# States, down products and steps of a two-layer streaming encoder moved and merged

## The chip, the cores and the metric

The kernel runs on one core of a Trainium2 chip. The metric is the device time of one execution in microseconds, the median of several runs. TensorE (PE in the profile) multiplies matrices, VectorE (DVE) and ScalarE (ACT) work element by element, GpSimd (POOL) does small element-wise work and issues some transfers, and SyncE (SP) issues nearly all transfers between device memory and the on-chip memory. "PEld" is TensorE's loading of the stationary operand, which overlaps its products.

## The reference

Two layers of an encoder advance by one step for 512 new frames of one stream and 16 frames of each of 8 running streams: 640 rows ("tokens") of width 1024 in all. Each layer is half a feed-forward network, a mixer, and another half feed-forward network, each wrapped in a layer norm. The change touches the feed-forward network and the second mixer:

```python
def swiglu(x, w_gate, w_up, w_down):
    return (jax.nn.silu(x @ w_gate) * (x @ w_up)) @ w_down

# second mixer (mixer_ssd), after proj = x @ w_in split in z, xbc, dt_raw
conv = conv_b + sum(ext[:, w:w + length] * conv_w[w] for w in range(SSD_CONV))
xbc = jax.nn.silu(conv)

# one chunk of its recurrence (ssd_recurrence)
cs = jnp.cumsum(dt_c * a, axis=1)
seg = cs[:, :, None] - cs[:, None]
decay = jnp.exp(jnp.where(causal, seg, -jnp.inf))
cb = jnp.einsum('btgn,bsgn->btsg', c_c, b_c)
w = cb[..., None] * decay * dt_c[:, None]
y = jnp.einsum('btsgr,bsgrp->btgrp', w, x_c)
y = y + jnp.einsum('btgn,bgrpn->btgrp', c_c, h) * jnp.exp(cs)[..., None]
to_end = jnp.exp(cs[:, -1:] - cs) * dt_c
h_new = h * jnp.exp(cs[:, -1])[..., None, None] + jnp.einsum('bsgr,bsgn,bsgrp->bgrpn', to_end, b_c, x_c)

# its output
yg = y * silu(z)
yg = yg * rsqrt(mean(yg ** 2) + RMS_EPS) * norm_g
out = yg @ w_out
```

There are 32 heads in 4 groups of 8; a head's state is 64 x 128. The hidden width of the feed-forward network is 2816, which is 22 tiles of 128. The new state `h_new` of the 8 running streams is an output of its own, and nothing else uses it.

## The kernel before

The six sub-layers run one after the other as stages: ffn0, mix0, ffn1, ffn2, mix1, ffn3. Every matrix product is made in three parts: each operand is split into a high part of reduced precision and a low rest, and `mm3` (lines 129 to 135) adds high x high, low x high and high x low in one bank. `split` (93 to 96) makes the parts, a copy on ScalarE and a subtraction on VectorE. `load_w` (111 to 118) loads a weight tile on SP's queue and splits it.

**Feed-forward network** (`ffn`, from 213). The 22 hidden tiles are handled as two alone and then twenty in pairs; gate and up products of a pair are formed by a scheme of seven block products in place of eight (`matrix`, with its products at line 358). After every four hidden tiles `down` multiplies them by their rows of the down matrix. In ffn1 and ffn2, which `SEVEN` (line 31) names, four of the six down blocks run as `down7`, again seven block products in place of eight (products at line 494). It needs sums of hidden rows (`row_sums`), differences of weight rows on VectorE (468 to 471), and part of its results is added to `yacc` by accumulating transfers on GpSimd's queue (506). The fifth token tile, the first block (two hidden tiles) and the last block stay in the plain form, `tm_proj`. In ffn3 all down blocks are plain: for each of five token tiles and two halves of the width, 12 products of 512 columns.

**Second mixer** (`mixer1`, from 1473). For each of 4 groups there are six tiles of convolved projections (`xbc`) and four of gate projections (`gate_in`). They go to device memory (`bcx_d`, `z_d`) and are reread in blocks of 128 tokens. Blocks 0 to 3 of a group are the 512 new frames, in chunks; block 4 holds the 16 frames of the 8 running streams. The order of blocks in a group is 4, 0, 1, 2, 3; one block of one group is a step, and there are 20. In each step come one projection tile of the next group (`run_fill`), `core_a` for the next step's block, `core_b` (or `core_s` for block 4), another projection tile, and `gate_out` for the same block of the group before, which multiplies by the gate (`zz`, line 1767), normalizes and projects out. In the last group no projections are left to fill in. After the last step come the five `gate_out` of the last group, each with a layer norm.

`xbc` convolves by windows: the 512 frames and the 8 runs of 16 frames are separate steps on ScalarE (1554) and VectorE (1557), three taps on VectorE, then Tanh (1558) and a last step (1559). `core_a` loads `bx` and `csb`, subtracts the decay of each of 8 heads in 8 steps on VectorE (1662), takes Exp of the whole (1664), and for block 4 writes its rows of x and B, split, to `xb_d` (1691, 1692). `core_s` loads the old states of the running streams (`load_h0`) for their part of the output. `gate_out` splits its result in four steps each on ScalarE (1780) and VectorE (1781), which also scale by `norm_g`.

**New states of the running streams** (`ssd_states`, 1445 to 1471) are made beside ffn3: for each of 16 pairs of streams and groups, 12 small loads bring rows from `xb_d` to `xrow` and `brow` (1459, 1460), the old states are loaded again, one product per state tile (1467) forms the update, and VectorE multiplies the old state (1469) and adds (1470). `tick` draws a step of it at five places in ffn3's loop over pairs.

**Queues.** Every engine takes its instructions in order. `issue_after(i)` puts what is traced in its block behind `i` on the engine of `i`, without a wait of its own.

**Start.** The first product is that of ffn0, as soon as the first weight and the first columns of x are split.

Of the kernel before, what the change touches and what calls it, by code (L numbers as in the profile page):

```python
# [9 lines left out]
F32 = mybir.dt.float32  # L10
# [11 lines left out]
T = 640  # L22
# [7 lines left out]
PAIRS = 6  # L30
SEVEN = ("ffn1", "ffn2")
PHASES = ("ffn0", "mix0", "ffn1", "ffn2", "mix1", "ffn3")
# [4 lines left out]
def kernel(ctx: ExitStack, tc: tile.TileContext, I, O, phases=PHASES):  # L37
# [91 lines left out]
    def mm3(ps, lhs, rhs):  # L129
        n = 3 * len(lhs)  # L130
        k = 0
        for (wh, wl), (xh, xl) in zip(lhs, rhs):
            for a, b in ((wh, xh), (wl, xh), (wh, xl)):
                state["pe"] = nc.tensor.matmul(ps, a, b, start=(k == 0), stop=(k == n - 1)).ins  # L134
                k += 1


# [75 lines left out]
    def ffn(i, ph, last, side=None):  # L213
# [4 lines left out]
        with ExitStack() as st:  # L218
# [1216 lines left out]

    ssd = {}

    def load_h0(wk, g, j):
# [3 lines left out]

    def ssd_states(wk):

        el8 = wk.tile([128, 4, 8, 8], F32, name="el8")
        nc.sync.dma_start(el8.rearrange("p g b h -> p g (b h)"), ssd["el"])


        xrow = wk.tile([128, 512], F32R, name="xrow", bufs=1)
        brow = wk.tile([128, 2, 128], F32R, name="brow", bufs=1)  # L1450
        nc.vector.memset(xrow.bitcast(F32), 0.0)
        nc.vector.memset(brow.bitcast(F32), 0.0)
        for g, b2, q in ((g, b2, q) for g in range(4) for b2 in range(2) for q in range(2)):
            for h in range(2):
                for r, (sx, sb) in enumerate(((0, 0), (0, 1), (1, 0))):
                    rows = slice(64 * h + 16 * r, 64 * h + 16 * r + 16)
                    t0 = 64 * h + 32 * b2 + 16 * q
                    src = lambda s, a, b: ssd["xb"][g][s, t0:t0 + 16, a:b]
                    nc.sync.dma_start(xrow[rows].bitcast(F32), src(sx, 0, 512))
                    nc.sync.dma_start(brow[rows, h].bitcast(F32), src(sb, 512, 640))  # L1460
            for h in range(2):
                n = 4 * h + 2 * b2 + q
                h0 = wk.tile([128, 512], F32, name="h0", bufs=2)
                nc.sync.dma_start(h0, I["ssd_h0"][g, n])
                yield
                pst = bank_b()
                nc.tensor.matmul(pst, brow[:, h], xrow, start=True, stop=True)  # L1467
                h4 = h0.rearrange("p (h d) -> p h d", d=64)
                nc.vector.tensor_tensor(h4, h4, el8[:, g, n, :, None].to_broadcast([128, 8, 64]), op=ALU.mult)
                nc.vector.tensor_tensor(h0, h0, pst, op=ALU.add)  # L1470
                nc.sync.dma_start(O["ssd_s"][g, n], h0)

    def mixer1(ph, last):
        V, G = nc.vector, nc.gpsimd
        cs_d = dram.tile([32, T], F32, name="cs_d")
        bcx_d = [dram.tile([128, NT, 6, 128], F32, name=f"bcx_d{g}") for g in range(4)]
        el_d = ssd["el"] = dram.tile([128, 4, 64], F32, name="el_d")
        xb_d = ssd["xb"] = [dram.tile([2, 128, 640], F32, name=f"xb_d{g}") for g in range(4)]
        z_d = [dram.tile([128, NT, 4, 128], F32, name=f"z_d{g}") for g in range(4)]
        with ExitStack() as st:  # L1480
# [58 lines left out]
            def xbc(g, u):  # L1539
                for h in range(0 if (g, u) not in xin else 1, 2):  # L1540
                    xbc_half(g, u, h)
                _, ext, m = xin[g, u]
                es_ = ext[:, 515:667].rearrange("p (b i) -> p b i", i=19)
                if u == 0:
                    cvo[g] = wk.tile([128, 6, 27], F32, name="cvo", bufs=1)
                G.tensor_copy(cvo[g][:, u, 0:3], ext[:, 512:515])
                G.tensor_copy(cvo[g][:, u, 3:27].rearrange("p (b i) -> p b i", i=3), es_[:, :, 16:19])
                if u == 5:
                    nc.sync.dma_start(O["conv"][:, 6 * g:6 * g + 6], cvo[g])
                acc = row_tile("acc")[:, :T]  # L1550
                win = lambda w: ((ext[:, w:w + 512], acc[:, 0:512]),
                                 (es_[:, :, w:w + 16], acc[:, 512:640].rearrange("p (b i) -> p b i", i=16)))
                for i_, o_ in win(0):
                    nc.scalar.activation(o_, i_, AF.Identity, scale=cw[:, m, 0:1], bias=cw[:, m, 4:5])
                for w in range(1, 4):
                    for i_, o_ in win(w):
                        V.scalar_tensor_tensor(o_, i_, cw[:, m, w:w + 1], o_, op0=ALU.mult, op1=ALU.add)
                nc.scalar.activation(ext[:, :T], acc, AF.Tanh)
                V.scalar_tensor_tensor(acc, ext[:, :T], 1.0, acc, op0=ALU.add, op1=ALU.mult)
                nc.sync.dma_start(bcx_d[g][:, :, u, :], acc.rearrange("p (c t) -> p c t", t=128))  # L1560

# [67 lines left out]

            bl = {}  # L1630

            def core_a(g, c):
                bx = wk.tile([128, 6, 128], F32, name="bx", bufs=2)
                nc.sync.dma_start(bx, bcx_d[g][:, c])
                bt, ct, xs = bx[:, 0], bx[:, 1], bx[:, 2:6]
# [9 lines left out]
                else:  # L1645
                    e8 = wk.tile([128, 8, 8], F32, name="e8")
                    nc.scalar.activation(e8.rearrange("p b h -> p h b"),
                                         csb.rearrange("p h (b i) -> p h b i", i=16)[:, :, :, 15], AF.Exp)
                    nc.sync.dma_start(el_d[:, g], e8.rearrange("p b h -> p (b h)"))
                ecs = None  # L1650
# [7 lines left out]
                elif c == 4:  # L1658
                    ecs = wk.tile([128, 8], F32, name="ecs8")
                    nc.scalar.activation(ecs, tok[:, c, 0, hs], AF.Exp)  # L1660
                for h in range(8):
                    V.tensor_scalar(csb[:, h, :], csb[:, h, :], tok[:, c, 0, 8 * g + h:8 * g + h + 1], 0.0,
                                    op0=ALU.subtract, op1=ALU.min)
                nc.scalar.activation(csb, csb, AF.Exp)
                pcb = bank_b()
# [64 lines left out]
            def core_s(g, c):  # L1730
# [9 lines left out]
                for j in range(4):  # L1740
                    h0 = load_h0(wk, g, j)
# [17 lines left out]
            def gate_out(g, c):  # L1759
                if g not in wo:  # L1760
                    wo[g] = [load_w(I["m1_out"][4 * g + k]) for k in range(4)]
                y = ys.pop((g, c))
# [14 lines left out]
                og = wk.tile([128, 4, 2, 128], F32R, name="csb" if g == 3 and c % 2 else "og", bufs=2 if g == 3 and c % 2 else 1)  # L1777
                for q in range(4):
                    ng = chp[:, 1, 4 * g + q:4 * g + q + 1]
                    nc.scalar.mul(og[:, q, 0], y[:, q], ng)  # L1780
                    V.scalar_tensor_tensor(og[:, q, 1], y[:, q], ng, og[:, q, 0].bitcast(F32),  # L1781
                                           op0=ALU.mult, op1=ALU.subtract)
                for j in range(2):
# [68 lines left out]

    open_banks()
    if "mix0" in phases and "ffn0" not in phases:
        with ExitStack() as st:
# [3 lines left out]
    if "mix0" in phases and "ffn0" in phases:  # L1859
        sides["ffn0"] = s5_tables  # L1860
    if "mix1" in phases and "ffn3" in phases:
        sides["ffn3"] = ssd_states
    for ph in phases:
# [5 lines left out]
        else:  # L1869
            mixer1(ph, last)  # L1870
            if "ffn3" not in phases:
                with ExitStack() as st:
                    for _ in ssd_states(pool("ssd", 1, st, reuse_waits="tile")):
                        pass
    banks[-1].close()
# [111 lines left out]
```

## Time and profile before

| | us |
|---|---|
| median of 3 runs | 2548.34 (2546.8 to 2552.1) |
| profiled execution, its time | 2548.97 |
| profiled execution, its span | 2547.3 |
| ffn0, from the span's start to its layer norm | 0 to 432 |
| second mixer with its layer norm | about 1597 to 2113 |
| ffn3 from there to its last down block | 2113 to 2511 |
| last down block and layer norm | 2511 to 2547 |

The page has engine totals, the chain of work that ended last, and groups of equal instructions with their mean duration and the idle time before them. The windows give each engine's busy time in a stretch. A matmul's duration contains its way through the array; what it costs in a dense stream is the distance from one start to the next, which is shorter. In the chain and the timeline the first number is the start in us from the span's start and the second is the length in us.

### The profile page before, as it was taken

To read this page: it belongs to the slowest core of one execution; us is meant where nothing else is said; L and a number is where in the kernel's file an instruction comes from. 1 tells how busy PE (TensorE), PEld (TensorE's weight loads), DVE (VectorE), ACT (ScalarE), POOL (GpSimd) and SP (SyncE) were. 2 spreads that over 40 slices of the span, in tenths; PEclk is the share of its full clock that TensorE was granted. 3 is DMA by queue.
4 is the path that set the end of the run, shared out by engine and by line. 5 is a ranking of instruction groups with operands and counts; after the bars stand their busy time and mean duration, and the time that the engine had idled before them with its cause. 6 is when DMAs were issued, how large, how long until landed. Compare 5 with 4: busy or idle time off the path is not lost. (4 is left out here: it accounts for less than half of the span.)

```text
span 2547.3 us, 40681 instructions
## 1 busy us (share of the span) xinstructions
PE 2501.8 (98%) x15577; PEld 2289.1 (90%) x15577; DVE 2017.0 (79%) x3685; ACT 1218.0 (48%) x2309; POOL 298.3 (12%) x432
## 2 busy tenths in 40 slices
PE   9999999999999999999999999999999999999998
PEld 8998999878789999999999999888989879999997
DVE  7787777676778888878888887777686799876768
ACT  4443344336744555553455554566565443443332
POOL 0000001210130000013000002311111150000001
PEclk9999999999999999999999999999999999999999
DMA  5322334443221433452144434366564722543442
GB/s 185 108 92 86 114 117 154 143 150 114 87 76 58 125 103 91 117 156 72 53 114 123 112 103 127 117 189 196 155 204 142 240 74 85 168 147 107 145 140 96
DMA packets 174835, 317.44 MB, mean 125 GB/s; under 512 B 20480, under 2 KB 91776, under 8 KB 174128
## 3 DMA queue, kind: packets, MB, share of 16 engines
q1 hardware_dynamic: 164816, 293.83, 36.2%
q0 software_dynamic: 9824, 21.01, 4.0%
q8 instruction: 122, 2.00, 0.3%
q14 instruction: 73, 0.60, 0.1%
HBM read 259.56 MB, written 40.54 MB: 118 GB/s over the span
## 5 line engine op out<-in xcount | busy, mean ns | idle before, releaser
L96 DVE TENSOR_TENSOR w<-raw,w 128x512 fp32r<-128x512 f32 (+1 forms) x601 | 524.1, 897 | 74.6 <-ACT w L95 73.3
L95 ACT CAST w<-raw 128x512 fp32r<-128x512 f32 (+1 forms) x601 | 441.7, 776 | 286.5 <-PE bank L134 102.7
L358 PE MATMUL bank<-xhi,w 128*128 128x320 f32 x2432 | 540.0, 309 | 1.5 <-ACT mx L369 1.1
L134 PE MATMUL bank<-xhi,w 128*128 128x256 f32 (+2 forms) x2272 | 497.3, 311 | 8.2 <-ACT w L95 6.2
L134 PE MATMUL bank<-w,h 128*128 128x512 f32 x1872 | 436.8, 392 | 0.0
L358 PE MATMUL bank<-T,w 128*128 128x320 f32 x2736 | 426.3, 309 | 1.1 <-DVE s L395 0.7
L134 PEld LDWEIGHTS bank<-w,h 128*128 128x128 f32 x1872 | 350.3, 188 | 73.2 <-DVE h L96 1.0
L358 PEld LDWEIGHTS bank<-xhi,w 128*128 128x128 f32 x2432 | 407.4, 188 | 5.4 <-ACT mx L369 2.3
L358 PEld LDWEIGHTS bank<-T,w 128*128 128x128 f32 x2736 | 406.4, 188 | 3.0 <-DVE s L395 1.3
L134 PEld LDWEIGHTS bank<-xhi,w 128*128 128x128 f32 x2272 | 377.6, 188 | 19.5 <-ACT w L95 6.2
L358 PE MATMUL bank<-xlo,w 128*128 128x320 f32 x1216 | 375.1, 308 | 0.0
L134 PE MATMUL bank<-xlo,w 128*128 128x256 f32 (+2 forms) x1136 | 350.6, 309 | 3.0 <-DVE xlo L198 2.9
L358 PEld LDWEIGHTS bank<-xlo,w 128*128 128x128 f32 x1216 | 228.0, 188 | 0.3
L134 PEld LDWEIGHTS bank<-xlo,w 128*128 128x128 f32 x1136 | 213.8, 188 | 4.4 <-DVE xlo L198 3.6
L210 DVE SCALAR_TENSOR_TENSOR yacc<-bank,yacc 128x512 f32<-128x512 f32 x160 | 109.3, 687 | 76.7 <-PE bank L134 76.2
L369 ACT COPY mx<-bank 128x320 f32<-128x320 f32 x228 | 96.5, 424 | 140.5 <-PE bank L358 140.1
L96 DVE TENSOR_TENSOR w<-sw,w 128x1024 fp32r<-128x1024 f32 x76 | 93.0, 1224 | 53.4 <-ACT w L95 53.0
L95 ACT CAST w<-sw 128x1024 fp32r<-128x1024 f32 x76 | 79.9, 1051 | 98.1 <-DVE sw L337 96.9
L506 POOL DMA_DIRECT2D yacc<-ev x56 | 48.7, 903 | 644.6 <-ACT ev L505 587.8
L134 PE MATMUL bank<-w,og 128*128 128x512 f32 x432 | 104.8, 396 | 2.8 <-DVE og L1781 2.8
L134 PEld LDWEIGHTS bank<-w,og 128*128 128x128 f32 x432 | 79.5, 188 | 20.7 <-DVE og L1781 4.7
L397 ACT ACTIVATE s<-s 128x320 f32<-128x320 f32 x108 | 50.9, 471 | 83.6 <-DVE s L395 83.4
(428 smaller groups left out, 3468.0 us busy)
## 6 DMA issues: line engine op xcount, KB each, us to landing
raw<-in_w_gate_dram SPq DMA_DIRECT2D x88, 512.0 KB, 3.9
raw<-in_w_up_dram SPq DMA_DIRECT2D x88, 512.0 KB, 4.0
raw<-in_w_down_dram SPq DMA_DIRECT2D x88, 512.0 KB, 3.6
raw<-in_m_in_dram SPq DMA_DIRECT2D x52, 512.0 KB, 4.5
yacc<-ev POOLq DMA_DIRECT2D x56, 256.0 KB, 4.3
raw<-in_m_out_dram SPq DMA_DIRECT2D x24, 512.0 KB, 4.1
csb<-cs_d SPq DMA_DIRECT2D x20, 512.0 KB, 5.0
h<-in_ssd_h_dram SPq DMA_DIRECT2D x16, 512.0 KB, 6.2
```

The lines of the kernel that those rows point to most:

```text
L95: nc.scalar.copy(hi, src)
L96: return nc.vector.tensor_tensor(lo, src, hi.bitcast(F32), op=ALU.subtract)
L134: state["pe"] = nc.tensor.matmul(ps, a, b, start=(k == 0), stop=(k == n - 1)).ins
L210: state["acc"] = nc.vector.scalar_tensor_tensor(ya, pb, scale, ya, op0=ALU.mult, op1=ALU.add).ins
L358: nc.tensor.matmul(ps, A[p][:, a, k * 128:k * 128 + 128], B[p][b][:, k, :], start=(first and n == 0), stop=(n == 11), skip_group_check=True)
L369: nc.scalar.copy(e[n], ps)
L397: state["silu"] = nc.scalar.activation(t, ps, AF.Silu).ins
L506: nc.gpsimd.dma_start(yacc[:, t, 512 * j:512 * j + 512], e, accum_op=ALU.add)
```

## The change

- ffn3 joins the stages with seven-product down blocks; the steps beside it go.
- The new states are made in the mixer: `states_in` loads rows, in the step of block 4 for four streams and in the step of block 1 for the other four, into two pairs of `xrow` and `brow`; `states_new` makes four states in the steps of block 0 and of block 2, from the old states that `core_s` loaded; `states_out` stores them a step later. Loads and stores stand behind the load of a block (`state["bx"]`) on SP's queue. The decay factors stay on the chip.
- The convolution runs over all 664 positions at once; positions between runs hold values that nothing reads. The result of the running streams goes to a tile of its own, and there are two stores.
- The eight decay subtractions become one, and the minimum with 0 becomes Relu on ScalarE.
- `norm_g` moves into the output weights (`load_w` with `rows`); the split of the gate's result is one step on each engine.
- Eleven products of the identity with itself stand ahead of the first product.

```diff
-SEVEN = ("ffn1", "ffn2")
+SEVEN = ("ffn1", "ffn2", "ffn3")
...
-    def load_w(src):
+    def load_w(src, rows=None):
...
-            split(w[:, j, 0], w[:, j, 1], r[:, 512 * j:512 * j + 512])
+            half = r[:, 512 * j:512 * j + 512]
+            if rows is None:
+                split(w[:, j, 0], w[:, j, 1], half)
+            else:
+                nc.scalar.mul(w[:, j, 0], half, rows)
+                nc.vector.scalar_tensor_tensor(w[:, j, 1], half, rows, w[:, j, 0].bitcast(F32),
+                                               op0=ALU.mult, op1=ALU.subtract)
...
-                state["pe"] = nc.tensor.matmul(ps, a, b, start=(k == 0), stop=(k == n - 1)).ins
+                with tc.issue_after(state["first"]) if "first" in state else ExitStack():
+                    state["pe"] = nc.tensor.matmul(ps, a, b, start=(k == 0), stop=(k == n - 1)).ins
...
-                elif ph == "ffn3" and where in ("gate", "up", 0, 2, 4):
-                    with tc.issue_after(state["silu"]):
-                        next(steps, None)
...
-                acc = row_tile("acc")[:, :T]
-                win = lambda w: ((ext[:, w:w + 512], acc[:, 0:512]),
-                                 (es_[:, :, w:w + 16], acc[:, 512:640].rearrange("p (b i) -> p b i", i=16)))
-                for i_, o_ in win(0):
-                    nc.scalar.activation(o_, i_, AF.Identity, scale=cw[:, m, 0:1], bias=cw[:, m, 4:5])
+                acc = row_tile("acc")
+                n = 664
+                nc.scalar.activation(acc[:, :n], ext[:, :n], AF.Identity, scale=cw[:, m, 0:1], bias=cw[:, m, 4:5])
                 for w in range(1, 4):
-                    for i_, o_ in win(w):
-                        V.scalar_tensor_tensor(o_, i_, cw[:, m, w:w + 1], o_, op0=ALU.mult, op1=ALU.add)
-                nc.scalar.activation(ext[:, :T], acc, AF.Tanh)
-                V.scalar_tensor_tensor(acc, ext[:, :T], 1.0, acc, op0=ALU.add, op1=ALU.mult)
-                nc.sync.dma_start(bcx_d[g][:, :, u, :], acc.rearrange("p (c t) -> p c t", t=128))
+                    V.scalar_tensor_tensor(acc[:, :n], ext[:, w:w + n], cw[:, m, w:w + 1], acc[:, :n],
+                                           op0=ALU.mult, op1=ALU.add)
+                nc.scalar.activation(ext[:, :n], acc[:, :n], AF.Tanh)
+                runs = lambda t: t[:, 515:667].rearrange("p (b i) -> p b i", i=19)[:, :, :16]
+                last_ = wk.tile([128, 128], F32, name="cvs", bufs=2)
+                V.scalar_tensor_tensor(last_.rearrange("p (b i) -> p b i", i=16), runs(ext), 1.0, runs(acc),
+                                       op0=ALU.add, op1=ALU.mult)
+                V.scalar_tensor_tensor(acc[:, :512], ext[:, :512], 1.0, acc[:, :512], op0=ALU.add, op1=ALU.mult)
...
+            def states_in(g, j):
+                x, b = xrow[j % 2], brow[j % 2]
+                for h in range(2):
+                    for r, (sx, sb) in enumerate(((0, 0), (0, 1), (1, 0))):
+                        rows = slice(64 * h + 16 * r, 64 * h + 16 * r + 16)
+                        t0 = 16 * (2 * j + h)
+                        with tc.issue_after(state["bx"]):
+                            nc.sync.dma_start(x[rows].bitcast(F32), xb_d[g][sx, t0:t0 + 16, 0:512])
+                            nc.sync.dma_start(b[rows, h].bitcast(F32), xb_d[g][sb, t0:t0 + 16, 512:640])
...
+            def states_new(g, j):
+                h0 = h0s.pop((g, j))
+                for h in range(2):
+                    n = 2 * j + h
+                    pst = bank_b()
+                    nc.tensor.matmul(pst, brow[j % 2][:, h], xrow[j % 2], start=True, stop=True)
+                    V.tensor_tensor(by_head(h0[:, h]), by_head(h0[:, h]), decay[g][:, n, :, None].to_broadcast(hb3),
+                                    op=ALU.mult)
+                    V.tensor_tensor(h0[:, h], h0[:, h], pst, op=ALU.add)
+                made.append((g, j, h0))
...
-                for h in range(8):
-                    V.tensor_scalar(csb[:, h, :], csb[:, h, :], tok[:, c, 0, 8 * g + h:8 * g + h + 1], 0.0,
-                                    op0=ALU.subtract, op1=ALU.min)
-                nc.scalar.activation(csb, csb, AF.Exp)
+                V.tensor_tensor(csb, csb, tok[:, c, 0, hs, None].to_broadcast([128, 8, 128]), op=ALU.subtract)
+                nc.scalar.activation(csb, csb, AF.Relu, scale=-1.0)
+                nc.scalar.activation(csb, csb, AF.Exp, scale=-1.0)
...
-                for q in range(4):
-                    ng = chp[:, 1, 4 * g + q:4 * g + q + 1]
-                    nc.scalar.mul(og[:, q, 0], y[:, q], ng)
-                    V.scalar_tensor_tensor(og[:, q, 1], y[:, q], ng, og[:, q, 0].bitcast(F32),
-                                           op0=ALU.mult, op1=ALU.subtract)
+                split(og[:, :, 0], og[:, :, 1], y)
...
+                states_out()
                 (core_b if c < 4 else core_s)(g, c)
+                if c == 1:
+                    states_in(g, 2)
+                    states_in(g, 3)
                 run_fill(0 if i in (8, 14) else 1)
+                if c == 4:
+                    states_in(g, 0)
+                    states_in(g, 1)
+                elif c in (0, 2):
+                    states_new(g, c)
+                    states_new(g, c + 1)
...
+    pw = bank_b()
+    for _ in range(11):
+        state["first"] = nc.tensor.matmul(pw[:, 0:128], ident, ident, start=True, stop=True).ins
```

More of the change, by code (lines that the diff above doesn't have):

```diff
@@ L133, in mm3 @@
             for a, b in ((wh, xh), (wl, xh), (wh, xl)):
-                state["pe"] = nc.tensor.matmul(ps, a, b, start=(k == 0), stop=(k == n - 1)).ins
+                with tc.issue_after(state["first"]) if "first" in state else ExitStack():
+                    state["pe"] = nc.tensor.matmul(ps, a, b, start=(k == 0), stop=(k == n - 1)).ins
                 k += 1
+        state.pop("first", None)
     xt = {n: act.tile([128, KT, T], F32R, name="x" + n) for n in ("hi", "lo")}
@@ L1441, in load_h0 @@
         return h0
[L1443 to L1471, printed above, removed]
     def mixer1(ph, last):
@@ L1476, in mixer1 @@
         bcx_d = [dram.tile([128, NT, 6, 128], F32, name=f"bcx_d{g}") for g in range(4)]
-        el_d = ssd["el"] = dram.tile([128, 4, 64], F32, name="el_d")
-        xb_d = ssd["xb"] = [dram.tile([2, 128, 640], F32, name=f"xb_d{g}") for g in range(4)]
+        xb_d = [dram.tile([2, 128, 640], F32, name=f"xb_d{g}") for g in range(4)]
         z_d = [dram.tile([128, NT, 4, 128], F32, name=f"z_d{g}") for g in range(4)]
@@ L1648, in core_a @@
                                          csb.rearrange("p h (b i) -> p h b i", i=16)[:, :, :, 15], AF.Exp)
[L1649 removed]
+                    decay[g] = e8
                 ecs = None
@@ L1760, in gate_out @@
                 if g not in wo:
-                    wo[g] = [load_w(I["m1_out"][4 * g + k]) for k in range(4)]
+                    wo[g] = [load_w(I["m1_out"][4 * g + k], chp[:, 1, 4 * g + k:4 * g + k + 1]) for k in range(4)]
                 y = ys.pop((g, c))
@@ L1870 @@
             mixer1(ph, last)
[L1871 to L1874, printed above, removed]
     banks[-1].close()
```

23 lines of the change are left out of this document (17 added, 6 removed).

## Prediction

> **What bounds the kernel now.** First the page: engine totals and the chain that ended last.
>
> ```profile
> span 2547.3 us, 40681 instructions
> PE 2501.8 (98%) x15577; PEld 2289.1 (90%) x15577; DVE 2017.0 (79%) x3685; ACT 1218.0 (48%) x2309; POOL 298.3 (12%) x432
> PE 15%; DVE 2%; DMA 0%; issue 0%; ACT 0%; POOLq 0%; DVEq 0%; ACTq 0%
> ```
>
> TensorE is busy for 98% of the span, and the chain of waits, as far as it reaches back, is mostly TensorE. So a removed product is worth its place in the stream, and a removed VectorE step is worth something only where TensorE stands idle. Next the windows, by stage: the second mixer and its end, then ffn2 and ffn3 between the same two marks (from the transposes of the last token tile of the norm before, to the first product of the last down block).
>
> ```profile
> 1610.00:2060.00 450.00, 444.58 (x2953) 400.53 (x2952) 336.59 (x763) 256.75 (x726) 73.09 (x162) 1.00 0.57 179
> 2060.00:2113.33 53.33, 50.15 (x284) 42.59 (x284) 48.80 (x95) 23.73 (x46) 29.82 (x29) 1.00 0.18 56
> 1187.83:1566.97 379.14, 378.76 (x2290) 357.67 (x2289) 321.96 (x497) 196.14 (x311) 25.41 (x30) 1.00 0.39 106
> 2113.33:2511.34 398.01, 396.49 (x2370) 372.98 (x2369) 309.02 (x488) 155.16 (x265) 1.15 (x2) 1.00 0.42 134
> ```
>
> The columns are length, then busy time of PE, PEld, DVE, ACT, POOL. ffn2 does with VectorE busy for 85% (321.96 of 379.14) and leaves TensorE 0.4 us idle. The second mixer leaves 5.4 us idle in 450 and 3.2 in its end. These idle times are all that VectorE's relief can win there.
>
> **ffn3 by seven products.** ffn2 is the price list: same sizes, already in the new form. TensorE's rows of the same two windows, by line: the plain product helper in ffn2 and ffn3, the seven-product line in ffn2, the state products in ffn3.
>
> ```profile
> 1187.83:1566.97 379.14, 67.44 (x350) 59.90 (x349) 1.00 0.39 106
> 2113.33:2511.34 398.01, 156.47 (x734) 132.15 (x733) 1.00 0.42 134
> 1187.83:1566.97 379.14, 77.95 (x336) 62.76 (x336) 1.00 0.39 106
> 2113.33:2511.34 398.01, 12.54 (x32) 6.00 (x32) 1.00 0.42 134
> ```
>
> ffn3 runs 734 plain products; ffn2 runs 350 and 336 in the new form, 686. That is 48 fewer: four down blocks, each 84+24 in place of 120. ffn3 also loses the 32 state products. What one costs in the stream is read from the chain, in order of time:
>
> ```profile
> 2385.12 10.88 PE bank L134 x48
> 2396.00 0.23 PE bank L1467
> ```
>
> 10.88/48 = 0.227 us for a product of 512 columns, 0.23 for a state product. So 48 x 0.227 = 10.9 and 32 x 0.23 = 7.4, together 18.3 us. The windows say the same: 398.01 - 379.14 = 18.9; the remaining 0.6 is idle time (1.5 us of TensorE in ffn3's window, 0.4 in ffn2's). I take **-18.9**. Its bounds are -18.3 (the idle time stays) and -18.9. What ffn3 gains in VectorE work (sums, differences, splits) and in accumulating transfers on POOL is what ffn2 carries already with 0.4 us of idle TensorE; if that cover were gone it would show there. The state steps' VectorE work leaves ffn3.
>
> **States in the second mixer.** The 32 products come back there, into a stage with TensorE 98.8% busy: 32 x 0.23 = **+7.4**. Around them:
>
> ```profile
> L1469 DVE TENSOR_TENSOR h<-h,el 128x512 f32<-128x512 f32 x32 | 21.9, 685 | 1.6 <-DMA h<-in_ssd_h_dram 0.9 <-DVE h L1470 0.7
> L1470 DVE TENSOR_TENSOR h<-h,bank 128x512 f32<-128x512 f32 x32 | 21.8, 680 | 8.7 <-PE bank L1467 8.7
> L1662 DVE TENSOR_SCALAR csb<-csb,tok 128x128 f32<-128x128 f32 x160 | 34.3, 282 | 16.7 <-ACT e L1647 9.6 <-ACT el L1644 6.9
> L1670 DVE TENSOR_TENSOR csb<-csb,cbm 128x1024 f32<-128x1024 f32 x20 | 24.7, 1235 | 0.3
> L1781 DVE SCALAR_TENSOR_TENSOR og<-yb,chp,og 128x128 fp32r<-128x128 f32 x72 | 27.3, 426 | 5.0 <-ACT og L1780 5.0
> L1557 DVE SCALAR_TENSOR_TENSOR acc<-ext,cw,acc 128x512 f32<-128x512 f32 (+1 forms) x144 | 69.2, 548 | 17.7 <-POOL cvo L1547 8.6 <-ACT acc L1554 8.0 <-DMA raw<-in_m_in_dram 1.1
> L1559 DVE SCALAR_TENSOR_TENSOR acc<-ext,acc 128x640 f32<-128x640 f32 x24 | 19.7, 819 | 2.1 <-ACT ext L1558 2.0
> L1664 ACT ACTIVATE csb<-csb 128x1024 f32<-128x1024 f32 x20 | 21.2, 1058 | 23.9 <-DVE csb L1662 16.7 <-DVE rms L1775 7.1
> ```
>
> VectorE, as recorded. States: +(21.9+21.8) = +43.7. Decay differences: eight of 282 ns become one of 1235, 20 x (2.26-1.24) = -20.4. Output split: four of 426 become one of about 685 (a 512-wide step, first row), 20 x (1.70-0.69) = -20.2. Convolution: a tap's two steps (512 and 128 wide, 2 x 548 ns) become one step of 664 columns, by the 640-wide row about 0.84, and the last step's 819 becomes two, 2 x 548: 24 x (3 x 0.26 - 0.28) = -12.0. Sum -8.9. Records of short steps overlap; were half of the 52.6 saved such overlap, the sum would be +17. So -9 to +17, on 336.6 of 450: 73 to 79%, below ffn2's 85%. ScalarE gains the Relu, 20 x 1.06 = 21 us, on 57%. Both are covered by TensorE's stream in groups 0 to 2; in the last group, without projections left to fill in, they lie bare. TensorE's longest wait in this stage, the total with its count and the longest piece:
>
> ```profile
> PE bank L134 <- DVE og L1781: 2.8, 3, 2.1
> ```
>
> The 2.8 falls in the last gate steps, where VectorE is nearly full and the merged split is shorter: between -2.8 (all goes) and +5.5, if the four state renewals of the last group's third block (4 x 1.37 on VectorE) all land ahead of a gate step. The row nearest is the merged split's own saving of 1.0 per block against one such wait of 2.1; I take **-0.7**. The norm scale moved into the weights puts the same number of steps of the same width on the same engines: nothing.
>
> **The transfers.** The 32 loads of old states beside ffn3 go, the mixer's own load is used again. The 192 small row loads move into the mixer, on SP's queue, 24 at a time, in the first and third steps of each group, behind the load of a block.
>
> ```profile
> L1459 SPq DMA_DIRECT2D xrow<-xb_d x96: 302/418/982, 2113.7 to 2470.2; - x96
> ...
> 1836.79 0.32 SPq L1767 DMA_DIRECT2D zz<-z_d  x1
> ...
> 1852.87 0.38 PE L1773 MATMUL bank<-ones,zz 128*128 128x2 f32 x2
> ...
> 2028.74 0.60 SPq L1767 DMA_DIRECT2D zz<-z_d  x1
> ...
> 2034.86 0.68 DVE L1768 TENSOR_TENSOR yb<-yb,zz 128x512 f32<-128x512 f32 x1
> ...
> 2039.33 0.38 PE L1773 MATMUL bank<-ones,zz 128*128 128x2 f32 x2
> ```
>
> 24 x 0.418 = 10.0 us of SP. Behind them can stand the gate's load (zz), weight loads, and stores. From zz's issue to the use on TensorE it is 16.1 us in a step of an earlier group and 10.6 in the last group; there the first use on VectorE comes 6.1 after the issue. Weight loads have four buffers ahead and the SP queue mostly waits for VectorE to free them. The row loads themselves wait for products a whole step back; their own products come about a step later, so TensorE should find the rows there. Bounds: 0 (hidden) to +23.6 (below); near is the first, since most gate loads have more than 10 us. I take **+1.0**.
>
> **Identity products.** The start, TensorE unless marked:
>
> ```profile
> 1.26 0.28 POOL masks.py:199 TENSOR_SCALAR_AFFINE_SELECT ident<-ident 128x128 f32<-128x128 f32 x1
> ...
> 11.31 0.63 PE L134 MATMUL bank<-xhi,w 128*128 128x256 f32 x2
> 11.74 0.41 PE L134 MATMUL bank<-xlo,w 128*128 128x256 f32 x1
> 11.95 0.58 PE L134 MATMUL bank<-xhi,w 128*128 128x256 f32 x2
> ...
> 12.49 0.39 PE L134 MATMUL bank<-xhi,w 128*128 128x256 f32 x2
> 12.72 0.28 PE L134 MATMUL bank<-xlo,w 128*128 128x256 f32 x1
> 12.83 0.39 PE L134 MATMUL bank<-xhi,w 128*128 128x256 f32 x2
> ...
> 9.32 2.42 ACT L95 CAST w<-raw 128x512 fp32r<-128x512 f32 x4 [0.65 <-DMA raw<-in_w_up_dram]
> 9.97 2.58 DVE L96 TENSOR_TENSOR w<-raw,w 128x512 fp32r<-128x512 f32 x4 [0.57 <-ACT w L95]
> ```
>
> Three products take 0.64 us up to 11.95 and 0.34 after it: half rate from the first product (6.15 us) for 5.8 us. The page's clock row says full speed there and doesn't show it. With the identity ready at 1.54, products can run before 6.15. But the second weight's first low half is ready only at 9.97 + 0.64 = 10.6, so its 24 products (8 x 0.34 = 2.7) end at 13.3 in place of 11.95 + 2.7 = 14.7: **-1.35**, held later, as the next weights have us of slack. Bounds: 0 (the identity, mostly zeros, doesn't raise the clock) and -2.9 (all of the cold half).
> [...]
>
> **Sum.** -18.9 + 7.4 - 0.7 + 1.0 - 1.35 = -12.55. The profiled execution took 2548.97 (span 2547.3, 1.7 around it): 2536.4. The median of the runs is 2548.34, 0.6 lower, and the runs spread over 5.3; I forecast **2536.0**.
>
> **Rivals.**
> 1. *Waits of a few us in the mixer's last group* (for: VectorE is nearly full there, 48.8 of 53.3; against: only two blocks take new states there). The 4 x 1.37 = 5.5 us bare in place of -0.7: 2542. Chance 0.20.
> 2. *SP's queue becomes the bound; slower than before.* The 24 transfers go ahead of the gate's load each time. In groups 1 and 2, of the 16.1 us from issue to use, the landing and the gate's own steps take about 8 (an estimate: the last group's 10.6, of which 6.1 are spent up to the first use, taken as 2 more than the landing needs), so a 10.0 us delay costs about 1.9, four times; in the last group 8, twice: 7.6 + 16 = 23.6 in place of 1.0, giving 2558.6. It decides from 13.6 us of stalls, 2.3 us in each of the six steps. For it: the queue takes its transfers in one order. Against: in the rows above the gate's load is issued ahead of the next block's load at times, so the order follows readiness. Chance 0.07.
> 3. *More than forecast:* VectorE's relief removes the waits for og and most of the 5.4 us idle: 3.5 to 5 us better, 2531.5. Against: part of that idle is the norm at the mixer's start. Chance 0.14.
> 4. *Relu doesn't share ScalarE's table with Exp and Tanh.* A load is 1.28 us:
>
> ```profile
> 11.76 1.28 ACT L273 ACT_TABLE_LOAD   x1
> ```
>
> Two per block put 2.6 us on each block's decay chain; bare in four blocks of the last group and in four latency-bound others, 20 us: 2556. Against: Copy, Identity and Square run today between Tanh and Exp, without loads in the groups. Chance 0.02.
> [...]
>
> **Chances and range.** Forecast 0.57, rivals 0.20, 0.07, 0.14, 0.02. About 0.2%, 5 us, is what can be told from no change: faster means below 2543.2. Forecast, rival 3 and about three quarters of rival 1 lie there: 0.86; same 0.06 (the rest of rival 1, milder stalls); slower 0.08. The range, 2529.5 to 2544.0, takes in rivals 1 and 3 with the spread of the runs, and leaves out 2 and 4 and their milder forms.
>
> **What would show it.** Right: ffn3 between its marks at about 379 us, with 336 products on the seven-product line and 350 plain ones; mixer from its first product to the same mark 7 to 8 us longer; full rate of TensorE from its first projections. Wrong: TensorE waiting in the mixer for state rows, for zz or for decay tiles; table loads in the blocks; ffn3 longer than ffn2. If the mixer grows by over 20 us, SP's queue took the gain.

## The result, and the profile after

The changed kernel takes 2612.94 us (median of 4 runs, 2611.73 to 2613.75), the kernel before 2548.2 in runs beside it: a ratio of 1.0253, 95% interval 1.0241 to 1.0266. It is slower by 65 us; 12 us faster was forecast.

From the page of the changed kernel, engine totals, the row of the granted clock in 40 slices, and the chain:

```profile
span 2610.0 us, 40449 instructions
PE 2508.9 (96%) x15551; PEld 2291.2 (88%) x15551; DVE 2045.2 (78%) x3511; ACT 1261.6 (48%) x2289; POOL 337.2 (13%) x464
PEclk9999999999999999999999999998989889999999
PE 29%; DVE 4%; DMA 2%; ACT 2%; POOL 1%; SPq 1%; issue 1%; POOLq 0%; DVEq 0%; ACTq 0%
```

TensorE is busy 7 us longer in all, though it has fewer products, and its share fell from 98 to 96%. The dips of the clock row (slices 28 to 33) all lie in the second mixer. The windows show where the time went: from ffn2's last down block to the transposes of the mixer's last token tile, and from there to ffn3's last down block. Columns: start and end, length, busy time of PE, PEld, DVE, ACT and POOL, granted clock, DMA share, GB/s. First before, then after:

```profile
1566.97:2113.33 546.36, 534.53 (x3461) 477.32 (x3460) 419.42 (x920) 298.27 (x798) 128.57 (x217) 1.00 0.51 158
2113.33:2511.34 398.01, 396.49 (x2370) 372.98 (x2369) 309.02 (x488) 155.16 (x265) 1.15 (x2) 1.00 0.42 134
```

```profile
1559.97:2195.03 635.06, 560.00 (x3493) 494.41 (x3492) 434.86 (x738) 304.48 (x736) 143.41 (x221) 0.94 0.50 156
2195.03:2574.27 379.24, 378.90 (x2291) 357.72 (x2290) 321.08 (x496) 193.67 (x307) 25.28 (x30) 1.00 0.38 104
```

ffn3 gave what was forecast: 379.24 - 398.01 = -18.8. Up to the mixer 7.0 us are won (1559.97 against 1566.97); the experiments below whose start is the same reach that mark at 1560.9 to 1564.8, so part of the 7.0 is spread between executions. The mixer grew by 88.7, and ate both: -7.0 + 88.7 - 18.8 - 0.2 (the end) = +62.7, the difference of the spans. In the mixer TensorE stands idle for 75.1 us (635.06 - 560.00) where it stood 11.8. The waits of TensorE, total, times and longest, name most of it:

```profile
PE bank L1785 <- POOL zz L1784: 54.3, 5, 17.6
PE bank L141 <- ACT w L121: 11.1, 1, 11.1
```

Five waits for the gate's squares (zz) and one for an output weight. The longest, in the timeline of all engines (start, length; in brackets the idle time before, and who ended it). Line numbers are those of the changed kernel: 1623 and 1624 are the row loads, 1779 the load of zz, 1647 that of bx, 1780 the product with the gate, 1781 and 1784 the squares and their sum, 1785 the product that adds them up.

```profile
2102.06 1.09 PE L1731 MATMUL bank<-csb,xd 128*64 128x128 f32 x16
2103.32 0.60 SPq L1623 DMA_DIRECT2D xrow<-xb_d  x1
2103.96 0.42 SPq L1624 DMA_DIRECT2D brow<-xb_d  x1
...
2113.83 0.42 SPq L1623 DMA_DIRECT2D xrow<-xb_d  x1
2114.30 0.42 SPq L1624 DMA_DIRECT2D brow<-xb_d  x1
2114.81 0.37 SPq L1779 DMA_DIRECT2D zz<-z_d  x1
2115.29 0.36 SPq L1647 DMA_DIRECT2D bx<-bcx_d  x1
...
2117.61 0.69 DVE L1780 TENSOR_TENSOR yb<-yb,zz 128x512 f32<-128x512 f32 x1 [10.21 <-DMA zz<-z_d]
2118.39 0.63 ACT L1781 ACTIVATE zz<-yb 128x512 f32<-128x512 f32 x1 [8.68 <-DVE yb L1780]
...
2120.74 0.59 PE L1785 MATMUL bank<-ones,zz 128*128 128x2 f32 x2 [17.59 <-POOL zz L1784]
```

From 2103.32 to 2114.72 SP issues nothing but row loads. Only then come the gate's load and the next block's, and behind zz's landing stand VectorE, ScalarE, GpSimd and at last TensorE. The wait's row names GpSimd, but the first in the line is the load.
These are 20 of the burst's 24 loads; its first was issued at 2096.5. From the first row load to the last, the six bursts that stand ahead of a gate's load take 18 to 23 us, not the 10.0 of 24 issues, because other transfers stand between the row loads, and some of them wait. In the burst from 2041.25 to 2064.38 the largest such wait of SP is for VectorE, ahead of two stores of gate projections (line 1555; the 8.2 is the total of the two):

```profile
SPq L1555 <- DVE acc L1548: 8.2, 2, 5.0
```

### The profile page after: what moved, and what is told of

Read it like the earlier page. It is cut to its first block, busy times and chain, and to the rows that moved or that the text cites. A ratio compares the mean times of both kernels' runs of the same rounds, so it can differ in the third digit from the quotient of the medians.

```text
span 2610.0 us, 40449 instructions
## 1 busy us (share of the span) xinstructions
PE 2508.9 (96%) x15551; PEld 2291.2 (88%) x15551; DVE 2045.2 (78%) x3511; ACT 1261.6 (48%) x2289; POOL 337.2 (13%) x464
## 5 line engine op out<-in xcount | busy, mean ns | idle before, releaser
L96 DVE TENSOR_TENSOR w<-raw,w 128x512 fp32r<-128x512 f32 (+2 forms) x569 | 520.3, 937 | 73.7 <-ACT w L95 72.7
L141 PE MATMUL bank<-w,h 128*128 128x512 f32 x1488 | 346.3, 391 | 0.0
L141 PEld LDWEIGHTS bank<-w,h 128*128 128x128 f32 x1488 | 276.9, 188 | 57.1 <-DVE h L96 1.0
L511 POOL DMA_DIRECT2D yacc<-ev x84 | 72.8, 892 | 965.9 <-ACT ev L510 884.4
L499 PE MATMUL bank<-w,hs 128*128 128x512 f32 x576 | 132.5, 389 | 0.0
L141 PE MATMUL bank<-w,og 128*128 128x512 f32 x432 | 118.9, 431 | 12.3 <-ACT w L121 11.1
L499 PEld LDWEIGHTS bank<-w,hs 128*128 128x128 f32 x576 | 108.1, 188 | 22.5
L141 PEld LDWEIGHTS bank<-w,og 128*128 128x128 f32 x432 | 89.1, 211 | 32.6 <-ACT w L121 11.8
```

Of the source, the lines that this page charges most:

```text
L96: return nc.vector.tensor_tensor(lo, src, hi.bitcast(F32), op=ALU.subtract)
L499: nc.tensor.matmul(ps, a[:, u], b[:, v], start=(first and n == 0), stop=(n == 5), skip_group_check=True)
L511: nc.gpsimd.dma_start(yacc[:, t, 512 * j:512 * j + 512], e, accum_op=ALU.add)
```

## The experiments

The kernel before, run beside each group of these, took 2546.7 to 2547.3 us. "The stretch" below is the mixer's window between the same two marks as above (546.4 before, 635.1 after).

### The row loads left out

```diff
-                for h in range(2):
+                for h in range(0):
                     for r, (sx, sb) in enumerate(((0, 0), (0, 1), (1, 0))):
```

> The changed kernel with the 192 row loads left out (the new states are then made of cleared rows; their values are not the reference's); products, VectorE steps, loads of old states and stores stay. Theory A (the row loads fill SP's queue, and the gate's load, the output weights and the block loads stand behind them): the stretch from ffn2's last down block to ffn3's last transposes falls from 635 to 550-556 us, the time to 2526-2534, waits of TensorE for zz near 0. Rival B (VectorE's 64 renewal steps and the longer decay chain with Relu make TensorE wait): the stretch stays above 610, the time above 2590.

One run: 2541.07 us. And the states left out altogether (`states_in`, `states_new`, `states_out` not called):

> The changed kernel with the new states of the running streams left out altogether (no row loads, products, VectorE steps or stores). A: 32 products of 0.23 us less than the run without row loads, so 2519-2527. B: near 2520 too, but then far below the run without row loads. Rival C (the merged steps themselves, the decay chain with Relu above all, slow the mixer): above 2560.

2526.62 us, ratio 0.9922 (0.9905 to 0.9938), so the rest of the change is worth 20 us. The stretch, with the row loads left out and with the states left out:

```profile
1564.21:2124.44 560.23, 545.03 (x3494) 485.13 (x3493) 432.33 (x738) 301.83 (x736) 160.90 (x221) 1.00 0.54 170
```

```profile
1560.88:2108.34 547.46, 534.71 (x3462) 478.32 (x3461) 395.11 (x674) 302.07 (x736) 144.89 (x221) 1.00 0.51 159
```

This splits the 88.7: +1.1 without states (547.46 against 546.36), +12.8 for the 32 products with their VectorE steps and stores (560.23), and **+74.8 for the 192 row loads** (635.06). Of the last, 59.9 is idle time of TensorE (75.1 against 15.2) and 15.0 is busy time for the same number of products, at a clock of 0.94 in place of 1.00. Leaving the loads out came 7 us above what was expected of it, since the 12.8 were taken for less.

### The same loads elsewhere in order, or on another queue

Queued behind the gate's load of their block:

```diff
-                        with tc.issue_after(state["bx"]):
+                        with tc.issue_after(state["zz"] if g else state["bx"]):
...
-                nc.sync.dma_start(zz, z_d[g][:, c])
+                state["zz"] = nc.sync.dma_start(zz, z_d[g][:, c]).ins
```

(`states_in` is called after `gate_out` for it.)

> The changed kernel with the same 192 row loads, traced after the gate's load of their step and put behind it on SP's queue. A, as an order of single loads: TensorE's waits for zz fall from 54 to under 15 us, the time to 2530-2560. Rival D (the small transfers load the DMA engines and so slow every other transfer, wherever they stand): the waits stay, above 2590.

2582.4 us, ratio 1.0137 (1.0122 to 1.0152): 30 us better than the change, but short of what was expected. TensorE's waits:

```profile
PE bank L141 <- ACT w L95: 10.0, 3, 4.6
PE bank L1785 <- POOL zz L1784: 8.2, 3, 4.0
PE bank L1678 <- DMA bx<-bcx_d: 4.4, 4, 1.7
```

zz fell from 54.3 to 8.2, and weights and bx are late in its place, as they would be if whatever stands behind the burst pays. The three rows are 22.6 of the 40.2 us for which TensorE stands idle in this run's stretch (602.19 - 561.97); 15.2 of idle time are there without row loads too.

Issued by ScalarE in place of SP:

```diff
-                            nc.sync.dma_start(x[rows].bitcast(F32), xb_d[g][sx, t0:t0 + 16, 0:512])
-                            nc.sync.dma_start(b[rows, h].bitcast(F32), xb_d[g][sb, t0:t0 + 16, 512:640])
+                        nc.scalar.dma_start(x[rows].bitcast(F32), xb_d[g][sx, t0:t0 + 16, 0:512])
+                        nc.scalar.dma_start(b[rows, h].bitcast(F32), xb_d[g][sb, t0:t0 + 16, 512:640])
```

> The changed kernel with the same row loads issued by ScalarE in place of SP. A: SP's queue is free and the gate's load in time; 192 issues of about 0.4 us take 80 us of ScalarE (58% busy in the mixer, then about 73%): 2530-2560. D: the transfers are the same, so above 2590.

2608.09 us, ratio 1.0237 (1.0222 to 1.0252). By its number this spoke against the queue as the cause. Its waits and its timeline say why it doesn't (line 1779 is here the product with the gate, on VectorE, and 1780 the squares, on ScalarE):

```profile
PE bank L1784 <- POOL zz L1783: 43.3, 4, 14.6
```

```profile
2098.22 0.69 DVE L1779 TENSOR_TENSOR yb<-yb,zz 128x512 f32<-128x512 f32 x1 [0.64 <-DMA zz<-z_d]
...
2106.47 0.63 ACT L1669 ACTIVATE ecs<-ecs 128x512 f32<-128x512 f32 x1 [5.76 <-DMA ecs<-cs_d]
2106.49 0.31 ACTq L1623 DMA_DIRECT2D brow<-xb_d  x1
...
2111.76 0.43 ACTq L1622 DMA_DIRECT2D xrow<-xb_d  x1
2112.23 0.43 ACTq L1623 DMA_DIRECT2D brow<-xb_d  x1
2112.70 0.63 ACT L1780 ACTIVATE zz<-yb 128x512 f32<-128x512 f32 x1 [5.60 <-DMA brow<-xb_d]
```

The gate's load is in time now, and the squares' input is ready at 2098.91, but the squares start only at 2112.70: in ScalarE's own order they stand behind the issues of the burst, and behind a load of ecs for which ScalarE waited 5.76. The block moved from the load of zz to its use. The theory had been told too narrowly: not SP's queue alone, but ScalarE's stream as well, when it carries the burst ahead of something that TensorE waits for (54.3 us of waits for zz with the burst on SP, 43.3 on ScalarE).
Issue time is what matters in this case: a row load takes 0.42 us to issue (median of 96, on SP) and 1.9 to land, and 24 of them stand in a line.

### Number of transfers against bytes

One load of 320 KB a pair (the expectation's 328, in the unit of its 240): the rows are stored already in the order of the product's partitions, with 8 stores a group in place of 2. A stream's product then runs over 64 partitions in place of 128 half cleared, and 16 that were cleared hold low x low.

```diff
+                    for k in range(4):
+                        nc.sync.dma_start(xb_d[g][:, k, :, 0:512], xs_[:, k // 2].bitcast(F32))
+                        nc.sync.dma_start(xb_d[g][:, k, :, 512:640], bs_[:, k % 2].bitcast(F32))
...
+                with tc.issue_after(state["bx"]):
+                    nc.sync.dma_start(xrow[j % 2].bitcast(F32),
+                                      xb_d[g][2 * j:2 * j + 2].rearrange("n k i c -> (n k i) c"))
```

> The split rows are stored in the order in which a step needs them (8 stores of a row group in place of 2), so that one load of 328 KB brings a pair's rows in place of 12 loads of 240 KB together: 16 row loads in all instead of 192, for more bytes. Theory Q (what costs is the number of transfers issued in order on a queue on which the gate's loads, the weights and the next block's loads also stand, 0.4 us each): 2536 to 2548 us, near the 2541 of the kernel without row loads, and no wait for zz over 3 us. Theory T (what costs is the traffic, that is bytes, engines or device memory): as slow as the change or slower, 2595 to 2625.

And the same layout and bytes, with that load cut into 12 (six ranges of rows, two of columns):

> As the run before, same layout and the same bytes, but the one load of a pair is cut into 12 by rows and columns, so 192 row loads stand on SP's queue again. Theory Q: the time returns to that of the change, 2595 to 2620 us, with waits of TensorE for zz of 10 us and over. Theory T (bytes), or that the scattered rows of the first layout were slow: within 8 us of the run before.

One load: 2578.48 us, ratio 1.0121 (1.0104 to 1.0139). Cut in 12: 2645.12 us, 1.0387 (1.0371 to 1.0402). TensorE's wait for zz, first of one load, then of 12:

```profile
PE bank L1777 <- POOL zz L1776: 15.9, 3, 8.6
```

```profile
PE bank L1779 <- POOL zz L1778: 58.3, 5, 16.7
```

At equal bytes, 176 more transfers cost 66.6 us, 0.38 each, close to the 0.42 of an issue: the number decides that much. But neither time was as expected: one load stays 37 us above the 2541 without row loads, and cut in 12 it is 32 us above the change. So this form costs some 30 us by itself, with few loads and with many. It stores twice the bytes with four times the stores (32 in all, which take SP 0.83 and 0.61 us each to issue, medians of 16) and loads a third more; which of these costs it was not tried.

### Fewer loads, smaller bursts

Four loads a pair from the change's own layout (partitions ordered by part, then stream; GpSimd masks the two streams apart), all else as in the change:

```diff
+                    nc.sync.dma_start(x[0:64].bitcast(F32), rows(0, 0, 512, [[0, 2]]))
+                    nc.sync.dma_start(x[64:96].bitcast(F32), rows(1, 0, 512, []))
+                    nc.sync.dma_start(b[0:64, 0].bitcast(F32), rows(0, 512, 128, [[128 * 640, 2]]))
+                    nc.sync.dma_start(b[64:96, 0].bitcast(F32), rows(0, 512, 128, []))
+                for h in (1, 0):
+                    G.tensor_scalar_mul(b[:, h], b[:, 0].bitcast(F32), half[:, h:h + 1])
```

> The change's layout in device memory and its 240 KB a pair kept, at the same places, but brought by 4 loads a pair in place of 12 (the partitions in another order, so that a load covers 32 or 64 of them; GpSimd then masks the two streams of a pair apart). 64 row loads in place of 192, bursts of 8 in place of 24. Theory Q (what stands in the way is the count of transfers issued in order): between the 2541 without row loads and the 2613 with 192 by their number, about 2565, 2555 to 2575. Theory T (bytes and device memory): 2600 and over.

2570.56 us, ratio 1.009 (1.0074 to 1.0105), as expected of the number. Then both with the four loads and with the change's twelve, one pair's rows a block and two products in the next:

```diff
-                if c == 4:
-                    states_in(g, 0)
-                    states_in(g, 1)
-                elif c in (0, 2):
-                    states_new(g, c)
-                    states_new(g, c + 1)
+                if c < 4:
+                    states_new(g, c)
+                if c != 3:
+                    states_in(g, (c + 1) % 5)
```

> As the run before, and one pair's rows a block (a burst of 4 loads, 1.7 us) with that pair's two products in the block after, in place of two pairs at once. Theory Q with slack (a burst costs only what exceeds the time by which zz is early): 2543 to 2556, at best 3 us faster than the kernel before. If the loss goes by the number of loads alone, it stays where the run before is, within 5 us.

> The change with its 12 loads a pair kept, but one pair's rows a block (bursts of 12, 5 us) and two products a block, as in the run before; 192 loads and the same bytes. Theory Q with slack: less is lost than in the change, 2565 to 2595, since a burst holds the gate's load back for half as long. If the number alone decides: 2605 to 2620.

Both leave out the store of the last pair of states of the last group (512 KB). Four loads spread: 2555.1 us, 1.0032 (1.0021 to 1.0043). Twelve loads spread: 2584.72 us, 1.0146 (1.0129 to 1.0163). Twelve loads at once and twelve spread are the same 192 transfers with the same bytes, in bursts of 24 and of 12; the second costs 28 us less. So the number of loads alone does not tell the loss; that a burst costs only what exceeds the time that its followers have to spare fits these times, but the spare time itself was not measured. Rival D, as it was put (above 2590 wherever the transfers stand), is out: the two kernels in which SP issues the 192 loads in another place or in smaller bursts took 2582.4 and 2584.72. A smaller cost of the transfers themselves is not excluded. TensorE's waits for zz follow the loss: four loads at once, twelve spread and four spread are 29, 44 and 14 us above the 2541 without row loads, the change 72 with 54.3 of waits.

```profile
PE bank L1793 <- POOL zz L1792: 26.7, 3, 15.1
PE bank L1785 <- POOL zz L1784: 38.5, 6, 11.9
PE bank L1793 <- POOL zz L1792: 6.7, 2, 4.7
```

Last, the four loads spread, with that store added, and beside it the same with the row loads queued behind the gate's load:

> Four loads a pair, one pair a block, as in the run of that order, with the one store added that was left out there (the states of the last pair of the last row group, 512 KB): 2553 to 2559 us, so 0.2 to 0.5% slower than the kernel before. It makes the best form of the change so far whole.

> As the run beside it, and the row loads are queued behind the gate's load of the same block. Theory Q: the 6.7 us of waits for zz go and up to 7 us are gained, 2546 to 2555, at best level with the kernel before. Rival (what is put behind the gate's load now holds back the next block's loads, as in the earlier run of that order): no gain, 2555 to 2565. Not expected by either: under 2541, which was the time with no row loads at all.

2554.54 us, 1.0027 (1.0015 to 1.0038), and 2548.39 us, 1.0004 (0.9995 to 1.0013): level with the kernel before. The stretch of the second, and its largest waits in the mixer:

```profile
1563.55:2128.85 565.30, 548.72 (x3494) 485.63 (x3493) 434.02 (x735) 301.15 (x732) 172.95 (x256) 0.99 0.57 175
```

```profile
PE bank L141 <- DVE og L96: 3.7, 2, 2.7
PE bank L1793 <- POOL zz L1792: 3.7, 2, 2.0
```

565.3 is 5.1 above the stretch without row loads: 70 of the 75 us are back. What remains above the kernel before's stretch, 18.9, is just what ffn3 won.

### The identity products alone

The kernel before, with the eleven products of the identity ahead of the first product and nothing else.

> The kernel before with nothing changed but the 11 identity products ahead of the first product. The prediction's term: -1.35 us, 2544.5 to 2547.5 where the kernel before takes 2546.7. Rival (the wait for the second weight takes all of it back): 0, within 0.5 us of the kernel before. A gain of over 3 us would mean that the clock does more at the start than was counted.

2543.71 us (11 runs) against 2546.9 (15 runs), ratio 0.9985 (0.9976 to 0.9994): faster by 3.2 us by the medians, by the interval between 1.5 and 6.1. Of the kernels here that leave nothing out, it alone is faster than the kernel before. Transposes of the first layer norm, first and last start, in the kernel before and in this one:

```profile
L196 PE MATMUL bank<-ident,yacc x200: 270/273/328, 443.7 to 2114.1; 128*128 128x128 f32 x100
```

```profile
L198 PE MATMUL bank<-ident,yacc x200: 270/273/328, 439.3 to 2108.6; 128*128 128x128 f32 x100
```

4.4 us are won before the first norm in these two executions, more than the 2.9 that the cold half of the start could give. The start itself shows less: by 20 us this kernel has run 101 products besides those of the identity, the kernel before 94, and 7 products at 0.34 for three are 0.8 us. Most of the rest is idle time of TensorE after 110 us, 4.0 us in the kernel before (333.70 - 329.69) and 1.4 in this one:

```profile
110.00:443.70 333.70, 329.69 (x1939) 303.55 (x1939) 265.28 (x578) 136.70 (x242) 22.65 (x26) 0.99 0.35 113
```

```profile
110.00:439.30 329.30, 327.94 (x1940) 302.38 (x1939) 265.12 (x578) 136.52 (x242) 22.65 (x26) 1.00 0.36 115
```

Whether that idle time hangs on the start or differs from execution to execution is not shown. The twelve other profiled kernels with these products reach the same transposes at 438.6 to 441.3.

Not tried: ffn3 by seven products with the states left beside it, and a second buffer for zz, with which the gate's load could go a block earlier.

## Why the prediction was wrong

- **ffn3, -18.9: right.** -18.8 between the marks. Its parts were a little off: by the prediction's own windows the 18.9 are 17.7 of busy time (396.49 - 378.76) and 1.1 of idle time, where it had 18.3 and 0.6.
- **The transfers, +1.0: the step that failed.** It read "near is the first, since most gate loads have more than 10 us" (from issue to use). That time is no reserve against a queue. The row loads don't eat into the way from zz's issue to its use, they put the issue itself off, by the 18 to 23 us of a burst and not by 10.0; and the distances of 16.1 and 10.6 us contained the landing and the gate's own steps. In its place the runs show +74.8: the number without row loads, the timeline, the cut load and the smaller bursts all point the same way.
- **Rival 2 was what happened, at a third of its size.** It had the mechanism, the place and even the count: six stalls, one at each burst that stands ahead of a gate's load. In groups 1 and 2 they measured 11.1 (for the output weight), 4.7, 11.9 and 5.3 us, priced at 1.9 each, and in the last group 14.8 and 17.6, priced at 8 each: 65.4 in all against 7.6 + 16 = 23.6. The price took 24 x 0.418 = 10.0 us for the delay, where the bursts took 18 to 23 with what stood between the row loads. Missing too were the loads beside zz that stand behind the same burst (bx and weights come up when zz is moved ahead), and the slower products after the stalls: the same products took 15.0 us longer. Its chance of 0.07 rested on "the order follows readiness". In the change the row loads stand behind the load of the next block, and in the timeline the burst goes as a whole ahead of the gate's load.
- **The 32 products, +7.4: mis-sized.** With the row loads left out TensorE's busy time is 10.3 us longer than without states (545.03 against 534.71), and the row of the 32 products has 10.1 of it:

```profile
1564.21:2124.44 560.23, 10.13 (x32) 5.79 (x32) 1.00 0.54 170
```

  The stretch grew by 12.8 for all that the states bring but row loads; the other 2.5 are idle time (15.2 against 12.75). Why a product costs 0.32 here and 0.23 beside ffn3 stays open.
- **VectorE's relief, -0.7: no gain.** Without states the stretch is 1.1 longer than before. The merged steps saved 24 us of VectorE's busy time (419.42 to 395.11) where 52.6 were counted; so about half of the recorded short steps had been overlap, the case of the prediction's upper bound. The busy times in the prediction's own rows say so beforehand: the 160 decay subtractions are 45.1 us by count and mean (160 x 0.282) and 34.3 by busy time, so their records overlap; reckoned from the four rows' busy times (34.3, 27.3, 69.2, 19.7), the same replacements save some 28 us. With the states VectorE rose by 15.4 (bound +17). TensorE still waited for og: 2.0 us at once without states, 2.8 in three waits in the kernel before.
- **The identity products, -1.35: too small.** Alone they give -3.2 (1.5 to 6.1), beyond the bound of -2.9, though the interval contains it. The start went as described in the changed kernel, where three of the first real products take 0.35 us from 6.78 on (though 0.74 from 7.25), and the second weight takes part back (a wait of 0.34 up to 10.38); with the identity products alone three take 1.12 us from 6.31 on, and 0.38 only from 7.88. What is won beyond the start, on the way to the first norm, has no shown cause.
- **Rivals 1, 3 and 4** did not come about. Rival 4: ScalarE's Relu (20 of 1.06 us) brought no table loads; between 1560 and 2200 us the trace has four, of 1.28 us each, as the kernel before has between 1560 and 2130.

## What to carry to other kernels

Count transfers by the time that their issue takes, and put the whole burst on the queue ahead of each load that stands behind it: 24 issues of 0.42 us are 10 us for everybody behind, and here 18 to 23 us with the transfers, and their waits, that stood between them. Beside ffn3 the same 192 loads had cost next to nothing (TensorE idle 1.5 us in that stage); that nothing urgent stood behind them there is the likely reason, but it was not tried. Another queue gave only 5 us here (2608.09 against 2612.94), since something urgent stood on it too, and that was compute: on ScalarE the burst held up the squares, ready at 2098.91, to 2112.70. Fewer and larger loads (42 us with four a pair), smaller bursts (28), and a place behind the urgent load (30) each brought part back, and together nearly all (65). A step that takes the long way from a load's issue to its use for slack should ask what decides the issue.

## What the runs showed of the hardware

**The stalls of TensorE were paid twice here.** The same kind of product in the changed kernel's timeline of TensorE, after the wait for an output weight and after the wait of 17.59 us:

```profile
1803.43 5.46 PE L141 MATMUL bank<-w,og 128*128 128x512 f32 x12 [11.15 <-ACT w L121]
...
2121.19 8.05 PE L141 MATMUL bank<-w,og 128*128 128x512 f32 x24
...
2135.77 3.89 PE L141 MATMUL bank<-w,og 128*128 128x512 f32 x16
```

After the first stall 12 products take 0.455 us each, twice the 0.227 of the dense stream in the prediction. After the second, 24 take 0.335 each, and 16 take 0.243 each 15 us later. Over the stretch the 2664 products of that line cost 12.7 us more than in the kernel with no row loads, first that kernel, then the change:

```profile
1564.21:2124.44 560.23, 452.15 (x2664) 407.95 (x2664) 1.00 0.54 170
```

```profile
1559.97:2195.03 635.06, 464.81 (x2664) 416.89 (x2664) 0.94 0.50 156
```

So 60 us of stalls beyond those of that kernel came with some 15 us of slower products, a quarter on top.
The granted clock has the same places. After the wait for the weight it is 0.60 from 1803.40 to 1810.00 and 1.00 from there to 1830.00; after the wait of 17.59 us it is 0.69 from 2121.00 to 2129.30 and 1.00 from there to 2140.00. Over the whole stretch, with its six stalls of 4.7 to 17.6 us, it is 0.94, and 1.00 in the kernel with no row loads.
